# A batched matmul on one core: TensorE's loop takes in the first tile, and a tenth pair of tiles is transposed on VectorE

## The chip, the cores and the metric

One core of one Trainium2 chip runs the whole program. The time is the device time of one execution in microseconds (us), as a median of several runs; the span of a profile is the time from the first to the last instruction of the one execution that was profiled, and is about 1.8 us shorter than that execution's time.

## The reference

```python
batch, m, k, n = 16, 512, 1024, 768
x          # [batch, m, k]  float32, normal
weight     # [k, n]         float32, normal
sub_value  # [batch, m, n]  float32, normal
return (np.matmul(x, weight) - sub_value).astype(np.float32)
```

With batch and m flattened there are 8192 rows, which is 64 **m tiles** of 128 rows. Each tile needs x in 16 bit, transposed (k on the partitions), then 16 weight loads and 16 matmuls of 128x384 (eight slices of k by two halves of n), then the subtraction.

## The kernel before

The kernel is written as one program for each engine, held in step by counting semaphores:

- SyncE (SP) starts all transfers, from one list, in order.
- ScalarE (ACT) casts each x tile to 16 bit, and copies TensorE's transposed tiles out of PSUM, the memory that TensorE writes to ("copy-out").
- For most tiles TensorE (PE) does the transpose: four instructions "T" per tile, two tiles ahead of their matmuls (the prediction writes T for all four). For some **pairs** of tiles VectorE (DVE) does it instead, in 16 instructions that handle 32x32 blocks of both tiles.
- VectorE also does each tile's subtraction, straight from PSUM.

TensorE's program repeats with a period of six tiles, a **lap**: four tiles of its own and one pair of VectorE's.

```python
ON_DVE = frozenset(range(10, 60, 6))     # nine pairs: 10-11, 16-17, ..., 58-59
LEAD_DVE, LEAD_TURN, PER = 7, 5, 6
LOOP = (4, 6, 10)                        # TensorE's loop: from tile 4, 6 tiles, 10 laps

def lead(mi):                            # how many tiles ahead ScalarE casts tile mi
    return LEAD_DVE if mi - mi % 2 in ON_DVE else TA + CA        # 7, else 4
...
for mi in range(HEAD + (EARLY is not None), n_mt):
    ...
    for c in range(n_c):                 # four chunks of k
        matmuls(mi, c)
        if tr:
            tr[c]()                      # one T of tile mi+2 after each chunk; the copy-out follows the fourth
    for t in range(max(mi, ahead), ...):
        if t - lead(t) == mi:
            cast(t)                      # ScalarE, behind the copy-out of this tile
    finish(mi)                           # VectorE's subtraction
    if mi + LEAD_TURN in ON_DVE:
        waiting += transposes_dve(mi + LEAD_TURN)
    for f in waiting[:PER]:              # VectorE: 6, 6 and 4 transposes behind three subtractions
        f()
    del waiting[:PER]
```

The order in which these calls are made is the order of the instructions on each engine. A pair waits for its second cast, TensorE's first weight load of a pair waits for the last of the 16 transposes, and tile t's output slot in PSUM is free when tile t-3 has been subtracted. Ahead of the loop stands a hand-made head that spreads tiles 0 to 2 over the arriving chunks of the weights.

## Time and profile before

| | before |
|---|---|
| time, median of 4 runs | 210.87 us (210.48 to 211.19) |
| span of the profile | 208.9 us |
| TensorE busy / VectorE / ScalarE | 94% / 61% / 52% |
| DMA queue, share of 16 engines | 97.7% |
| bytes moved | 61.87 MB read, 25.17 MB written |
| start of tile 4's matmuls / of tile 10's | 25.61 / 44.00 us |
| one lap in the steady part | 17.34 us |
| end of the matmuls / of the last subtraction / of the span | 201.2 / 202.2 / 208.9 us |

A page gives shares of the whole span, which say who is full but not who waits for whom. So the questions are put to the timeline: what does a lap consist of, and what was each engine released by. The lines are in the prediction below. In them, "[2.08 <-PE po_b L198]" after a row means that the engine had been idle for 2.08 us before it, and that the matmuls of line 198 ended that.

### The profile page before, as it was taken

To read this page: it belongs to the slowest core of one execution; us is meant where nothing else is said; L and a number is where in the kernel's file an instruction comes from. 1 tells how busy PE (TensorE), PEld (TensorE's weight loads), DVE (VectorE), ACT (ScalarE), POOL (GpSimd) and SP (SyncE) were. 2 spreads that over 40 slices of the span, in tenths; PEclk is the share of its full clock that TensorE was granted. 3 is DMA by queue.
4 is the path that set the end of the run, shared out by engine and by line. 5 is a ranking of instruction groups with operands and counts; after the bars stand their busy time and mean duration, and the time that the engine had idled before them with its cause. 6 is when DMAs were issued, how large, how long until landed. Compare 5 with 4: busy or idle time off the path is not lost.

```text
span 208.9 us, 2614 instructions
## 1 busy us (share of the span) xinstructions
PE 196.7 (94%) x1234; PEld 75.4 (36%) x700; DVE 127.8 (61%) x224; ACT 108.8 (52%) x113; POOL 1.0 (0%) x7
## 2 busy tenths in 40 slices
PE   6999799989999999999999999999999999999950
PEld 0234244333434434433443443343344344334310
DVE  2323316955993995596499299369749929943330
ACT  4364768507664671762844767173584655525300
POOL 1000000000000000000000000000000000000000
PEclk9999999999999999999999999999999999999996
DMA  6999999999999999999999999999999999999992
GB/s 238 406 426 433 440 420 436 449 431 430 433 458 414 353 446 445 446 414 411 475 419 422 438 414 438 461 425 422 431 447 397 436 442 438 414 438 442 411 417 119
DMA packets 5620, 87.08 MB, mean 417 GB/s; under 512 B 624, under 2 KB 624, under 8 KB 2032
## 3 DMA queue, kind: packets, MB, share of 16 engines
q1 hardware_dynamic: 5616, 87.03, 97.7%
q8 instruction: 1, 0.02, 0.0%
q14 instruction: 3, 0.02, 0.0%
HBM read 61.87 MB, written 25.17 MB: 417 GB/s over the span
## 4 chain that ended last, share of the span: by engine, by line
PE 72%; DMA 18%; SPq 4%; ACT 1%; issue 1%; DVE 0%
PE po_b L198 65%; DMA x_ring<-in_x_dram 18%; PE pt_b L335 7%; SPq L298 3%; SPq L262 1%; ACT xt_b L348 0%; DVE so_ring L417 0%; ACT x_b L317 0%; SPq L553 0%; ACT x16p_b L317 0%; SPq L138 0%
## 5 line engine op out<-in xcount | busy, mean ns | idle before, releaser
L198 PE MATMUL po_b<-w_sb,xt_b 128*128 128x384 f16 x704 | 126.0, 326 | 0.3 <-ACT xt_b L348 0.2
L417 DVE TENSOR_TENSOR so_ring<-po_b,so_ring 128x768 f32<-128x768 f32 x64 | 60.4, 956 | 58.6 <-PE po_b L198 37.4
L348 ACT COPY xt_b<-pt_b 128x1024 f16<-128x1024 f16 x44 | 44.5, 1012 | 64.2 <-PE pt_b L335 63.2
L368 DVE STREAM_TRANSPOSE xtp_b<-x16p_b 32x256 f32<-32x256 f32 x144 | 62.7, 435 | 3.3 <-ACT x16p_b L317 1.1
L198 PE MATMUL po_b<-w_sb,xtp_b 128*128 128x384 f16 x320 | 61.4, 326 | 1.0 <-DVE xtp_b L368 0.9
L397 PEld LDWEIGHTS <-xt_b 128*128 128x128 f16 x352 | 34.4, 98 | 57.7 <-issue 53.6
L317 ACT CAST x_b<-x_ring 128x1024 f16<-128x1024 f32 x46 | 47.2, 1048 | 4.3 <-DMA x_ring<-in_x_dram 4.3
L335 PE MATMUL pt_b<-ident,x_b 128*128 128x128 f32 x184 | 47.6, 274 | 1.6 <-ACT x_b L317 1.4
L335 PEld LDWEIGHTS pt_b<-ident,x_b 128*128 128x128 f32 x184 | 25.3, 141 | 46.0 <-issue 41.3
L317 ACT CAST x16p_b<-x_ring 128x1024 f16<-128x1024 f32 x18 | 18.8, 1046 | 16.8 <-DMA x_ring<-in_x_dram 16.8
L397 PEld LDWEIGHTS <-xtp_b 128*128 128x128 f16 x160 | 15.7, 98 | 19.9 <-issue 17.8
L265 DVE CAST w_sb<-so_ring 128x768 f16<-128x768 f32 x8 | 4.1, 556 | 11.4 <-DMA so_ring<-in_weight_dram 11.4
L198 PE MATMUL po_b<-idle_x,idle_w 128*128 128x512 f16 x26 | 8.8, 495 | 1.7 <-POOL idle_x L178 1.7
L348 ACT COPY xtp_b<-pt_b 128x1024 f16<-128x1024 f16 x2 | 2.0, 1012 | 2.1 <-PE pt_b L335 2.1
L317 ACT ACT_TABLE_LOAD x1 | 1.3, 1283 | 0.9 <-SPq L138 0.9
L427 PEld LDWEIGHTS <-idle_w 128*128 128x128 f16 x4 | 0.4, 99 | 1.7 <-POOL idle_x L178 1.7
L187 DVE TENSOR_TENSOR ident<-along,across 32x32 f32<-32x32 f32 x4 | 0.7, 183 | 0.1
L179 DVE MEMSET ones<- 128x32 f32 x1 | 0.1, 85 | 1.0 <-SPq L138 1.0
L178 POOL MEMSET idle_x<- 128x512 f16 x1 | 0.5, 528 | 0.0
L499 ACT CAST stub<-ident 128x1 f16<-128x1 f32 x2 | 0.4, 195 | 0.0
L184 DVE STREAM_TRANSPOSE across<-along 128x32 f32<-128x32 f32 x1 | 0.2, 212 | 0.0
L476 POOL MEMSET mark<- 128x1 f32 x1 | 0.1, 99 | 23.6 <-ACT xtp_b L348 23.6
(7 smaller groups left out, 1.0 us busy)
## 6 DMA issues: line engine op xcount, KB each, us to landing
so_ring<-in_sub_value_dram SPq DMA_DIRECT2D x7, 3072.0 KB, 24.2
x_ring<-in_x_dram SPq DMA_DIRECT2D x5, 4096.0 KB, 23.8
out_dram<-so_ring SPq DMA_DIRECT2D x6, 3072.0 KB, 29.2
x_ring<-in_x_dram SPq DMA_DIRECT2D x2, 2048.0 KB, 27.0
so_ring<-in_weight_dram SPq DMA_DIRECT2D x4, 768.0 KB, 8.2
x_ring<-in_x_dram SPq DMA_DIRECT2D x1, 3072.0 KB, 28.6
out_dram<-so_ring SPq DMA_DIRECT2D x1, 2688.0 KB, 26.5
x_ring<-in_x_dram SPq DMA_DIRECT2D x2, 1024.0 KB, 24.8
```

Source lines behind the costliest of these rows:

```text
L178: pool.add(lambda: nc.gpsimd.memset(idle_x, 0.0), then=count("idle"))
L187: dve.add(lambda here=here: nc.vector.tensor_tensor(out=ident[here, here], in0=along[here], in1=across[here], op=mybir.AluOpType.is_equal, ...
L198: return nc.tensor.add_instruction(mybir.InstMatmult(name=nc.get_next_instruction_name(), engine=full.engine, ins=list(full.ins), outs=lis ...
L262: sp.add(lambda st=st, at=at: nc.sync.dma_start(out=st, in_=w_c[at]), then=(sem, 16))
L265: lambda at=at, r=r, st=st: nc.vector.tensor_copy(out=w_sb[:, at, r], in_=st[:, r]),
L298: sp.add(lambda here=here, there=there: nc.sync.dma_start(out=here, in_=there), waits, (sem, 16))
L317: act.add(lambda: nc.scalar.copy(out=to, in_=x_in), waits, count("cast"))
L335: pe.add(lambda: nc.tensor.transpose(words, from_, ident), waits, count("turn") if last else None)
L348: act.add(lambda: nc.scalar.copy(out=to, in_=pt_b[:, b]), waits, count("evac"))
L368: dve.add(lambda: nc.vector.transpose(xt[b * Q : (b + 1) * Q, :, a * Q : (a + 1) * Q], x16[a * Q : (a + 1) * Q, :, b * Q : (b + 1) * Q],), ...
L397: pe.add(lambda weights=weights: nc.tensor.ldweights(weights, tile_position=(0, 0)), [w for w in waits if w[0] in ready])
L417: dve.add(lambda: nc.vector.tensor_tensor(out=o, in0=po[:, :, :NS], in1=o, op=mybir.AluOpType.subtract), [landed["s", mi], (counter["mul"] ...
```

## The change

The intent: a shorter TensorE program (254 instructions, instead of a head, a loop and a tail), in which tile 0 already belongs to the loop. Each turn has a block of four own tiles and a block of the pair; the last turn leaves after the first block. Tiles 4 and 5 become a tenth pair, the hand-made head goes, w2 and w3 are loaded earlier, and the four T of a tile come together, after the third chunk.

A loop in TensorE can wait on a counter only if the counts grow by the same step in every turn. With tile 0 in the loop this means that ScalarE has to cast the tiles in an order which keeps the counter "cast" in step from the first turn on. The change gets that by casting both tiles of a pair at the end of the tile before VectorE begins with them, so that all casts are in the order of the tiles. The diff, shortened and with its lines regrouped:

```diff
-LEAD_DVE = 7
+TURN_AT = 2
 LEAD_TURN = 5
-ON_DVE = frozenset(range(10, 60, 6))
-LOOP = (4, 6, 10)
+PERIOD, ON_PE = 6, 4
+ON_DVE = frozenset(range(4, 60, 6))
 TRANSFERS = [
-    ('x', 0, 1), ('w', 0, 1), ('x', 1, 1), ('w', 1, 1), ('x', 2, 1), ('w', 2, 1),
-    ('x', 3, 2), ('w', 3, 1), ('s', 0, 1), ('x', 5, 3), ('s', 1, 3), ('x', 8, 4), ...
+    ('x', 0, 1), ('w', 0, 1), ('x', 1, 1), ('w', 1, 1), ('w', 2, 1), ('x', 2, 1),
+    ('w', 3, 1), ('x', 3, 1), ('x', 4, 2), ('s', 0, 1), ('x', 6, 2), ('s', 1, 3), ('x', 8, 4), ...
... (emit_loop with one body becomes emit_turns with two blocks and two branches; the head goes) ...
+    casts = {0: [3, 4, 5]}
+    for mi in range(6, n_mt):
+        casts.setdefault(mi - mi % PERIOD + PERIOD - 1 - PERIOD if on_dve(mi) else mi - TA - 2, []).append(mi)
...
         for c in range(n_c):
             matmuls(mi, c)
-            if tr:
-                tr[c]()
+            if c == TURN_AT and mi + TA < n_mt and not on_dve(mi + TA):
+                transpose_tile(mi + TA)
+        for t in sorted(casts.get(mi, [])):
+            cast(t)
         finish(mi)
-        if mi + LEAD_TURN in ON_DVE:
-            waiting += transposes_dve(mi + LEAD_TURN)
-        for f in waiting[:PER]:
+        for t in range(mi + 1, n_mt):
+            if t in ON_DVE and mi == max(t - LEAD_TURN, 0):
+                waiting += transposes_dve(t)
+        for f in waiting[: 16 if mi < PERIOD - 1 else PER]:
             f()
```

## The prediction

> **What bounds the kernel now.** I read the page first, then the chain that ended last in order of time, then the timeline of each engine over the head and over one lap of TensorE's loop (six m tiles). A tile is 128 rows of x; a pair is two tiles whose transpose VectorE does; T is a tile's four TensorE transposes.
>
> ```profile
> PE 196.7 (94%) x1234; PEld 75.4 (36%) x700; DVE 127.8 (61%) x224; ACT 108.8 (52%) x113; POOL 1.0 (0%) x7
> DMA  6999999999999999999999999999999999999992
> ```
>
> Two resources are full at once: TensorE is 94% busy, and the DMA engines are at 90% or more in nearly every slice. VectorE and ScalarE seem to have room, but only on average.
>
> ```profile
> 9.99 38.47 DMA x_ring<-in_x_dram
> ...
> 57.09 5.85 PE po_b L198 x36
> ...
> 74.43 5.85 PE po_b L198 x36
> ...
> 91.78 5.85 PE po_b L198 x36
> ```
>
> The chain hangs on an x transfer until 48.5 us and on TensorE afterwards. The long pieces (tiles that carry no T) return every 17.34 us: that is a lap. It equals the work: 96 matmuls at 0.1625 (4 in 0.65) are 15.6, and 16 transposes at 0.108 (0.758 - 0.65 between their neighbours) are 1.73; sum 17.33. So laps cost nothing but arithmetic. A tile with T takes 3.03 us, one without 2.60. The waits of TensorE's loads between 60 and 201 us are all on "issue", at most 0.3 us each: no data wait is left. A lap moves 6 x (0.524 + 2 x 0.393) = 7.86 MB, at about 433 GB/s 18.15 us, longer than 17.34: the DMA queue carries a backlog, and the matmuls end at 201.2, the last stores at 208.
>
> Now the pair of such a lap, from the timeline of VectorE and TensorE (start, duration, engine):
>
> ```profile
> 68.29 0.96 DVE L417 TENSOR_TENSOR so_ring<-po_b,so_ring 128x768 f32<-128x768 f32 x1 [2.08 <-PE po_b L198]
> 69.16 2.66 DVE L368 STREAM_TRANSPOSE xtp_b<-x16p_b 32x256 f32<-32x256 f32 x6
> 71.84 0.96 DVE L417 TENSOR_TENSOR so_ring<-po_b,so_ring 128x768 f32<-128x768 f32 x1
> 72.83 2.68 DVE L368 STREAM_TRANSPOSE xtp_b<-x16p_b 32x256 f32<-32x256 f32 x6
> 75.53 0.96 DVE L417 TENSOR_TENSOR so_ring<-po_b,so_ring 128x768 f32<-128x768 f32 x1
> 76.52 1.80 DVE L368 STREAM_TRANSPOSE xtp_b<-x16p_b 32x256 f32<-32x256 f32 x4
> ...
> 79.47 0.81 PE L198 MATMUL po_b<-w_sb,xtp_b 128*128 128x384 f16 x4
> ```
>
> VectorE needs 9.16 us for a pair (69.16 to 78.32), with two subtractions in between, and starts right after the subtraction of tile 17. TensorE wants the pair at 79.47. **The slack is only 1.15 us**; the pair's casts were done at 68.32, before they were needed.
>
> **What the Trainium skill says.** (1) "TensorE: Matmul & The Clock Gate", Architectural detail: only TensorE reorders (weight loads), ScalarE and VectorE are strict first in, first out. The trace agrees: ScalarE idled 7.58 us before the cast at 48.49, and a finished TensorE transpose was copied out only afterwards, at 49.44. So program order on those engines counts. (2) The same page, The HAM clock gate: idle for a window of about 3.4 us halves the clock. Here the granted clock fell to 0.50 by 205 us, after the last matmul at 201.2; gaps of 1.4 us around 22 us left it at 1.00. (3) "Runtime: NRT & Kernel Launch", Instruction fetch mechanics: 256 instructions are one fetch block, and a branch out of the resident blocks stalls. The old loop shows no stall (17.34 against 17.33), so a 254-instruction program has nothing to win in the laps. (4) "DMA: Bandwidth & Descriptors", Where 436 GB/s comes from: a ceiling of 435 GB/s. The slices of 420 to 440 agree.
>
> **The change, part by part.**
>
> *Transposes moved.* Tiles 4 and 5 go from TensorE to VectorE: 184 transposes become 176, 8 x 0.108 = 0.9 us less TensorE, 16 x 0.445 = 7.1 us more VectorE.
>
> *T after the third chunk, four in a row.* Same cost (0.43), and the result is ready earlier in the tile.
>
> *The loop* now covers all tiles, with blocks of four and two and two branches a lap. Queued matmuls hide these, as in the old loop: about 0.
>
> *The head.* It no longer spreads tiles 0 to 2 over the arriving weights; w2 and w3 are loaded earlier instead. Transfer times, from the old landings:
>
> ```profile
> 16.94 1.03 DVE L265 CAST w_sb<-so_ring 128x768 f16<-128x768 f32 x2 [3.29 <-DMA so_ring<-in_weight_dram]
> 24.38 2.69 DVE L417 TENSOR_TENSOR so_ring<-po_b,so_ring 128x768 f32<-128x768 f32 x3 [4.55 <-DMA so_ring<-in_sub_value_dram]
> 25.61 0.81 PE L198 MATMUL po_b<-w_sb,xtp_b 128*128 128x384 f16 x4 [0.16 <-issue]
> ```
>
> 5.77 MB had landed at 16.9 and 8.91 at 24.4: 0.425 MB/us. In the new order w3 is in at 4.72 MB = 14.45 us, x4 and x5 at 6.29 MB = 18.15. Tile 0 ends at 16.2 (last w cast 15.5 plus a chunk), tile 1 at 19.2, tile 2 at 21.8, tile 3 at 24.4. But tile 4 needs its pair and, for its output slot, the subtraction of tile 1. ScalarE casts tiles 4 and 5 by 20.2. VectorE then does all 16 transposes in one run, 20.24 + 7.15 = 27.4, and only then subtracts tile 1: 28.4. Tile 4 starts at **28.45 instead of 25.61**: 2.8 us late, after a TensorE gap of 4.0 us.
>
> *The casts of the pairs.* This is the part that I think decides. The old code cast a pair 7 tiles ahead, one cast in each of two tiles. The new code puts both casts at the end of the tile before the one where VectorE begins, behind the copy-out of that tile's T and one other cast. Durations on ScalarE from the old trace:
>
> ```profile
> 17.50 0.60 PE L335 MATMUL pt_b<-ident,x_b 128*128 128x128 f32 x4
> 18.13 1.01 ACT L348 COPY xt_b<-pt_b 128x1024 f16<-128x1024 f16 x1 [1.99 <-PE pt_b L335]
> ...
> 57.18 1.01 ACT L348 COPY xt_b<-pt_b 128x1024 f16<-128x1024 f16 x1 [2.02 <-PE pt_b L335]
> 58.09 1.99 ACT L317 CAST x_b<-x_ring 128x1024 f16<-128x1024 f32 x2
> ...
> 41.96 1.79 DVE L368 STREAM_TRANSPOSE xtp_b<-x16p_b 32x256 f32<-32x256 f32 x4
> ...
> 44.00 0.81 PE L198 MATMUL po_b<-w_sb,xtp_b 128*128 128x384 f16 x4 [0.88 <-DVE xtp_b L368]
> ```
>
> From the start of tile 5 (of tile 11, and so on): 12 matmuls 1.95; T until its copy starts 0.63 (17.50 to 18.13); copy until the first cast 0.91; two casts at a spacing of 0.945, 1.89; the last cast 1.05; hand-over 0.04: VectorE starts at +6.47, where the old order would have let it start at about +4.0 (tile end 3.03 plus a subtraction). Then 9.16 for the pair and 0.25 until a matmul (41.96 + 1.79 to 44.00): +15.88. TensorE would be there at 3 x 3.03 + 2 x 2.60 = +14.3. So it **waits about 1.55 us in each lap**. This does not heal: tile 11 starts 3.03 after tile 10, so the lap is 18.9 us instead of 17.34, a closed ring TensorE, ScalarE, VectorE, TensorE, slower than the DMA's 18.15.
>
> *Sum.* Tile 5 starts at 28.45 + 3.03 = 31.48, tile 10 at 47.35 (old: 44.00), tile 11 at 50.4, tile 59 eight laps later at 201.6. Tiles 59 to 61 (3.03 each) and 62, 63 (2.60) end at 215.9; the old end was 201.2, so 14.7 later. The last subtraction ends at 216.9. In the old run the span ended 6.7 us after it, of which about 3 us were DMA backlog; that backlog is gone, since the DMA has caught up. I take 4.6 us: 3.3 as an empty queue's first load took, 1.4 from landing to the end. Span 221.5, plus 1.8 (210.7 against 208.9): 223.3. I predict **223 us**.
>
> **Rivals.** (a) *DMA stays the bound.* The bytes and their order after x6 are unchanged and DMA is full everywhere; if the new waits hid in its backlog, 208 to 213 us. Against it: 14.7 us is more than the backlog of 3 to 6 us, and the output of the last tile can't go before its matmuls. (b) *Only the head costs*: if the casts came in time, the 2.8 us would partly hide behind x16, which lands at 48.5: 211 to 214. It needs VectorE to start 1.5 us sooner than I compute; the order of the instructions on ScalarE speaks against it. (c) *Better*: 0.9 us of TensorE and fewer instructions to fetch, 208 to 210. TensorE isn't alone on the path, so even without any wait little comes of it. (d) *Worse*: the 4.0 us gap halves the clock for a window (1.7 us), or a branch to the second block misses a fetch; 225 to 228.
>
> **Range and chances.** The per-lap wait is a difference of two sums; an error of 0.4 us in it makes 9 x 0.4 = 3.6 us, and the head is good to 1 us. So 218 to 227.5 us. Slower by over 2% (over 215.1) 0.92; within 2% 0.06; faster 0.02.
>
> **What would show it.** Right: TensorE idles once a lap before the first pair matmul, released by VectorE's transposes; laps of 18.9 us; VectorE's first transposes of a pair released by ScalarE's cast of the pair; a gap of about 4 us before tile 4 with 16 transposes in a row; DMA slices under 90% late in the run; matmuls ending near 216. Wrong: laps of 17.3 or of 18.15 with x loads as releasers, or tile 4 before 27 us.

## The result, and the profile after

| | before | after |
|---|---|---|
| time, median of 4 runs | 210.87 us (210.48 to 211.19) | 223.64 us (222.38 to 223.99) |
| span of the profile | 208.9 us | 220.5 us |
| start of tile 4 / of tile 10 | 25.61 / 44.00 | 28.46 / 47.30 |
| one lap | 17.34 | 18.85 (one of eight: 19.16) |
| end of the matmuls / last subtraction / span | 201.2 / 202.2 / 208.9 | 215.9 / 216.9 / 220.5 |

The changed kernel is slower: ratio 1.06, 95% interval 1.056 to 1.064. (Here and below a ratio is one of mean times, so it is not quite the ratio of the medians.)

The page of the changed kernel, busy times, the DMA engines in 40 slices and the shares of the chain that ended last:

```profile
PE 196.2 (89%) x1217; PEld 71.5 (32%) x691; DVE 135.4 (61%) x240; ACT 105.9 (48%) x109; POOL 0.9 (0%) x6
...
DMA  6999999999999999999999999997999999939085
...
DVE 39%; PE 31%; ACT 16%; DMA 6%; issue 5%; SPq 2%; ACTq 0%
```

TensorE is as long busy as before, in a longer span. The DMA engines, full to the end before, now have slices at 70%, 30% and 0%: they stand still at times, and no longer set the end alone. The chain of before hung on DMA and then on TensorE alone; now VectorE and ScalarE hold more than half of it. VectorE is no busier as a share (61% both times), and still it stands on the path. The waits, in total, times and longest, name the links:

```profile
DVE xtp_b L365 <- ACT x16p_b L320: 21.2, 9, 2.6
...
PE po_b L201 <- DVE xtp_b L365: 12.4, 9, 1.6
```

Nine times VectorE waited for ScalarE's cast of a pair, and nine times TensorE waited for VectorE's transposes of it: once for each of the pairs from 10-11 on. (L345 is the copy-out, L320 the casts, L365 VectorE's transposes, L411 the subtraction, L201 the matmuls.) One lap in the timeline, ScalarE, then VectorE, then TensorE:

```profile
34.13 1.01 ACT L345 COPY xt_b<-pt_b 128x1024 f16<-128x1024 f16 x1 [1.07 <-PE pt_b L338]
35.04 1.05 ACT L320 CAST x_b<-x_ring 128x1024 f16<-128x1024 f32 x1
35.99 1.99 ACT L320 CAST x16p_b<-x_ring 128x1024 f16<-128x1024 f32 x2
...
38.01 2.67 DVE L365 STREAM_TRANSPOSE xtp_b<-x16p_b 32x256 f32<-32x256 f32 x6 [2.33 <-ACT x16p_b L320]
...
45.37 1.80 DVE L365 STREAM_TRANSPOSE xtp_b<-x16p_b 32x256 f32<-32x256 f32 x4
...
47.30 2.11 PE L201 MATMUL po_b<-w_sb,xtp_b 128*128 128x384 f16 x12 [1.34 <-DVE xtp_b L365]
66.15 2.11 PE L201 MATMUL po_b<-w_sb,xtp_b 128*128 128x384 f16 x12 [1.34 <-DVE xtp_b L365]
85.00 2.11 PE L201 MATMUL po_b<-w_sb,xtp_b 128*128 128x384 f16 x12 [1.34 <-DVE xtp_b L365]
104.16 2.11 PE L201 MATMUL po_b<-w_sb,xtp_b 128*128 128x384 f16 x12 [1.65 <-DVE xtp_b L365]
```

The copy-out waits for TensorE's T of this tile; behind it stand one own cast and the two casts of the pair; VectorE, free since 35.7, idles 2.33 us until the second is done at 37.98; it needs 9.16 us (38.01 to 47.17); and TensorE idles 1.34 us before the pair's first matmul. The starts repeat every 18.85 us. In the head, tile 4 starts only when VectorE has done 16 transposes in one run and then the subtraction of tile 1:

```profile
20.24 7.18 DVE L365 STREAM_TRANSPOSE xtp_b<-x16p_b 32x256 f32<-32x256 f32 x16
27.45 2.69 DVE L411 TENSOR_TENSOR so_ring<-po_b,so_ring 128x768 f32<-128x768 f32 x3
...
15.55 5.28 PE L201 MATMUL po_b<-w_sb,xt_b 128*128 128x384 f16 x16 [1.17 <-DVE w_sb L268]
...
28.46 2.11 PE L201 MATMUL po_b<-w_sb,xtp_b 128*128 128x384 f16 x12 [0.99 <-DVE so_ring L411]
```

The row at 15.55 is a surprise: 16 matmuls in 5.28 us are 0.33 us each, half speed. The granted clock was 0.50 from about 14.6 to 21.4 us. It fell after short TensorE gaps of 2.02, 1.04 and 0.42 us, within the one of 1.17. It cost no time here, because tile 4 waits for VectorE anyway; it only turned most of the gap before tile 4 into slower work.

Where the 11.6 us of span come from: tile 10 starts 3.3 us later; the eight laps from there to tile 58 take 151.1 us (7 x 18.85 + 19.16) instead of 139.5 (the first old one was 18.1, tile 16 at 62.1, then 7 x 17.34), 11.6 more; together 14.9, against 14.7 measured at the end of the matmuls. The tail from the last subtraction to the end of the span is 3.6 us instead of 6.7, which gives 3.1 back. (The median time grew by 12.8 us: the profiled run was the fastest of the changed kernel's.)

### The profile page after: what moved, and what is told of

Its sections match the earlier page's. It is cut to its first block, busy times and chain, and to the rows that moved or that the text cites. A ratio compares the mean times of both kernels' runs of the same rounds, so it can differ in the third digit from the quotient of the medians.

```text
span 220.5 us, 2621 instructions
## 1 busy us (share of the span) xinstructions
PE 196.2 (89%) x1217; PEld 71.5 (32%) x691; DVE 135.4 (61%) x240; ACT 105.9 (48%) x109; POOL 0.9 (0%) x6
## 4 chain that ended last, share of the span: by engine, by line
DVE 39%; PE 31%; ACT 16%; DMA 6%; issue 5%; SPq 2%; ACTq 0%
DVE xtp_b L365 31%; PE po_b L201 26%; ACT x16p_b L320 9%; DVE so_ring L411 8%; DMA x_ring<-in_x_dram 6%; PE pt_b L338 4%; ACT x_b L320 4%; ACT xt_b L345 3%; SPq L265 1%; SPq L301 1%; ACTq L55 0%; SPq L506 0%; SPq L143 0%
## 5 line engine op out<-in xcount | busy, mean ns | idle before, releaser
L201 PE MATMUL po_b<-w_sb,xt_b 128*128 128x384 f16 x704 | 122.6, 330 | 2.2 <-DVE w_sb L268 2.2
L345 ACT COPY xt_b<-pt_b 128x1024 f16<-128x1024 f16 x44 | 44.5, 1012 | 97.8 <-PE pt_b L338 97.8
L411 DVE TENSOR_TENSOR so_ring<-po_b,so_ring 128x768 f32<-128x768 f32 x64 | 60.3, 956 | 47.7 <-PE po_b L201 40.7
L365 DVE STREAM_TRANSPOSE xtp_b<-x16p_b 32x256 f32<-32x256 f32 x160 | 69.7, 436 | 23.7 <-ACT x16p_b L320 21.2
L201 PE MATMUL po_b<-w_sb,xtp_b 128*128 128x384 f16 x320 | 56.9, 326 | 13.4 <-DVE xtp_b L365 12.4
L320 ACT CAST x_b<-x_ring 128x1024 f16<-128x1024 f32 x44 | 45.1, 1048 | 5.2 <-DMA x_ring<-in_x_dram 5.2
L338 PE MATMUL pt_b<-ident,x_b 128*128 128x128 f32 x176 | 27.0, 276 | 2.4 <-ACT x_b L320 2.4
L338 PEld LDWEIGHTS pt_b<-ident,x_b 128*128 128x128 f32 x176 | 22.1, 143 | 18.0 <-ACT x_b L320 11.8
L320 ACT CAST x16p_b<-x_ring 128x1024 f16<-128x1024 f32 x20 | 19.9, 1045 | 1.4 <-DMA x_ring<-in_x_dram 1.4
L201 PE MATMUL po_b<-idle_x,idle_w 128*128 128x512 f16 x17 | 5.5, 472 | 1.7 <-POOL idle_x L181 1.7
```

The source lines that it names most:

```text
L201: return nc.tensor.add_instruction(mybir.InstMatmult(name=nc.get_next_instruction_name(), engine=full.engine, ins=list(full.ins), outs=lis ...
L320: act.add(lambda: nc.scalar.copy(out=to, in_=x_in), waits, count("cast"))
L338: pe.add(lambda: nc.tensor.transpose(words, from_, ident), waits, count("turn") if last else None)
L345: act.add(lambda: nc.scalar.copy(out=xt_b[:, d], in_=pt_b[:, b]), waits, count("evac"))
L365: dve.add(lambda: nc.vector.transpose(xt[b * Q : (b + 1) * Q, :, a * Q : (a + 1) * Q], x16[a * Q : (a + 1) * Q, :, b * Q : (b + 1) * Q],), ...
L411: dve.add(lambda: nc.vector.tensor_tensor(out=o, in0=po[:, :, :NS], in1=o, op=mybir.AluOpType.subtract), [landed["s", mi], (counter["mul"] ...
```

## The experiments

The theory: ScalarE's order places the casts of a pair too late, and this closes a ring (TensorE's T, copy-out, three casts, 16 transposes, the pair's matmuls) that is longer than both TensorE's own lap and the DMA's. The rivals: VectorE is overloaded by the tenth pair; the two-block program or its branches cost; the new head costs; ScalarE just has too much to do.

Three of the kernels (e1, e2, e6) need the pairs' casts in another order than that of the tiles. So in these the casts of the pairs count on a semaphore of their own ("castp"), and TensorE waits only on own tiles, whose casts stay in order.

### Control: the semaphore alone (e0_split)

```diff
-        act.add(lambda: nc.scalar.copy(out=to, in_=x_in), waits, count("cast"))
-        cast_at[mi] = so_far["cast"]
+        cast_on[mi] = "castp" if first in ON_DVE else "cast"
+        act.add(lambda: nc.scalar.copy(out=to, in_=x_in), waits, count(cast_on[mi]))
+        cast_at[mi] = so_far[cast_on[mi]]
... (VectorE's pairs wait on "castp"; a reload of x's ring waits on both) ...
```

> Control for the two runs that needed a semaphore of their own for the pairs' casts: the changed kernel with that semaphore and nothing else, ScalarE's order untouched. Theory: the semaphore is neutral, laps of 18.85 us, time 222.5 to 224.5. If the semaphore and not the place of the casts had helped, the time would come down towards 211 to 215.

Measured: 224.39 us (223.78 to 225.11), ratio to before 1.065; laps of 18.85 us, one of 19.16. The semaphore is neutral within 0.4%, where the loss is 6%. In this trace the half clock fell on tile 4 and tile 10 started at 48.62, 1.3 us later than in the profile of the changed kernel. That profile was the fastest of its runs (222.38 us; the others had 223.60 to 223.99), so the same accident may make this difference; it was not traced in those runs.

### The casts seven tiles ahead (e1_casts_seven_ahead)

```diff
 (on top of the control)
-        casts.setdefault(mi - mi % PERIOD + PERIOD - 1 - PERIOD if on_dve(mi) else mi - TA - 2, []).append(mi)
+        casts.setdefault(mi - 7 if on_dve(mi) else mi - TA - 2, []).append(mi)
```

> The changed kernel, but the casts of a VectorE pair come seven tiles ahead, one in each of two tiles, as in the old kernel (they count on a semaphore of their own, so that TensorE's loop can still wait by a fixed step). All else stays: head, ten pairs, two-block loop, four transposes in a row. Theory (casts too late on ScalarE): the wait of 1.3 us before each pair goes, laps of 17.35 us, tile 4 still at 28.5, matmuls end near 202, time 210 to 213, no more than 1% above the old kernel. Rival (VectorE overloaded by the tenth pair, or the two-block program and its branches): laps stay at 18.85 us, time 222 to 224. Rival (the head is what costs): time about 213.7.

Measured: 211.16 us (210.63 to 211.36), ratio 1.0008 (0.999 to 1.0025). The timeline of TensorE:

```profile
28.41 4.00 PE L201 MATMUL po_b<-w_sb,xtp_b 128*128 128x384 f16 x12 [3.85 <-DVE so_ring L415]
...
48.44 2.11 PE L201 MATMUL po_b<-w_sb,xtp_b 128*128 128x384 f16 x12
...
65.79 2.11 PE L201 MATMUL po_b<-w_sb,xtp_b 128*128 128x384 f16 x12
```

No idle time is left before the pairs (no bracket at 48.44 and 65.79), and the lap is 17.35 us. The tenth pair, the head, T in a block, both branches and the 254 instructions are all still there, so none of them is the cause of the longer laps. The gap of 3.85 us before tile 4 is there as well, and tile 4 after it ran at half clock (12 matmuls in 4.00 us instead of 2.11); tile 10 starts 4.4 us later than in the old kernel, the matmuls end at 204.7, 3.5 us later, and the time is the same. So the head's delay is real and costs nothing: it lies inside the DMA's backlog. The matmuls ended later than the expected 202, by this half clock: tiles 4 to 9 took 20.03 us (28.41 to 48.44) instead of 17.35, 2.7 more.

### A smaller dose: the pair ahead of the own cast (e2_pair_before_own)

```diff
 (on top of the control)
-        for t in sorted(casts.get(mi, [])):
+        for t in sorted(casts.get(mi, []), key=lambda t: (mi >= PERIOD - 1 and not on_dve(t), t)):
```

> The changed kernel, the two casts of a pair put ahead of the one own cast of the same tile, still behind that tile's copy-out; own semaphore for the pairs. A smaller dose. Theory: VectorE starts 0.945 us earlier in each lap, the wait of TensorE falls from 1.5 to 0.55 us, laps of 17.9 us; nine laps save 8.5 us of TensorE, matmuls end near 207, time 213 to 215. Rivals (VectorE's load, the program's form): 222 to 224, laps of 18.85.

Measured: 215.56 us (215.35 to 216.77), ratio 1.024, just above the expected 213 to 215. TensorE:

```profile
47.84 2.11 PE L201 MATMUL po_b<-w_sb,xtp_b 128*128 128x384 f16 x12 [0.40 <-DVE xtp_b L369]
65.75 2.11 PE L201 MATMUL po_b<-w_sb,xtp_b 128*128 128x384 f16 x12 [0.40 <-DVE xtp_b L369]
```

The idle time before a pair fell from 1.34 to 0.40 us, and the lap from 18.85 to 17.91: 0.94 us, one cast's spacing, as expected. The half clock met tile 4 here too (12 matmuls in 3.66 us), which is 1.55 us more than the 2.11 of full speed and puts all later tiles back by as much: that is about the miss.

### T after the first chunk (e3_turn_after_first)

```diff
-TURN_AT = 2
+TURN_AT = 0
```

> The changed kernel with one number changed: TensorE's four transposes come after the first of a tile's four chunks, not after the third, so that ScalarE's copy-out, and the casts that stand behind it, come 1.3 us earlier. No cast moves in ScalarE's order. Theory (the ring TensorE transposes, copy, three casts, pair, matmuls): wait per lap 1.5 - 1.3 = 0.2 us, laps of 17.6 us, time 210 to 214. Rival (ScalarE or VectorE simply has too much to do in a lap): no change, 222 to 224.

Measured: 210.84 us (210.69 to 212.45), ratio 1.0022 (0.998 to 1.0064). VectorE's first transposes of a pair in this kernel, and TensorE's first matmuls of tiles 10 and 16:

```profile
54.34 2.68 DVE L365 STREAM_TRANSPOSE xtp_b<-x16p_b 32x256 f32<-32x256 f32 x6 [1.03 <-ACT x16p_b L320]
...
46.09 0.81 PE L201 MATMUL po_b<-w_sb,xtp_b 128*128 128x384 f16 x4
63.64 0.81 PE L201 MATMUL po_b<-w_sb,xtp_b 128*128 128x384 f16 x4
```

Not one instruction of ScalarE moved in its order; only TensorE's T moved to another place in its tile. VectorE's wait for the cast fell from 2.33 to 1.03 us, by 1.30, the two chunks of 0.65 by which T moved. Laps are 17.55 us (46.09 to 63.64), 0.2 above 17.34 as expected, and the time lies in the expected 210 to 214. The load of ScalarE and VectorE is that of the changed kernel, so "too much to do" falls; the ring stands.

### The old kernel with late casts (e4_before_casts_late)

```diff
 (on the kernel before)
     def lead(mi):
-        return LEAD_DVE if mi - mi % 2 in ON_DVE else TA + CA
+        return 5 + mi % 2 if mi >= n_mt or mi - mi % 2 in ON_DVE else TA + CA
...
-            if t - (lead(t) if t < n_mt else LEAD_DVE) == mi:
+            if t - lead(t) == mi:
```

> The old kernel with nothing but the casts of the pairs moved to the tile and place where the changed kernel has them (fifth and sixth tile ahead, behind that tile's copy-out and one own cast). Old head, nine pairs, old loop. Theory: the loss comes by this alone, and a little more than in the changed kernel, since the old copy-out comes 0.65 us later in the tile: laps of 19.6 us, matmuls end near 219.7, time 224 to 228. Rival (new loop, new head or tenth pair cause the loss): the old kernel's time, 210 to 212.

Measured: 233.52 us (232.70 to 234.34), ratio 1.1065. The cause is right, the size was missed by 5.5 us beyond the range. TensorE:

```profile
87.47 0.81 PE L198 MATMUL po_b<-w_sb,xtp_b 128*128 128x384 f16 x4 [2.15 <-DVE xtp_b L368]
...
107.08 1.44 PE L198 MATMUL po_b<-w_sb,xtp_b 128*128 128x384 f16 x4 [2.10 <-DVE xtp_b L368]
...
128.38 0.81 PE L198 MATMUL po_b<-w_sb,xtp_b 128*128 128x384 f16 x4 [2.14 <-DVE xtp_b L368]
```

The lap from 87.47 to 107.08 is 19.61 us, as expected; the next is 21.30. In it four matmuls took 1.44 us instead of 0.81. The stretches of the trace around it (length, busy times of TensorE, its weight loads, VectorE, ScalarE and GpSimd, then the granted clock, DMA share and GB/s):

```profile
105.00:106.00 1.00, 0.00 (x0) 0.00 (x0) 0.94 (x4) 0.00 (x0) 0.00 (x0) 1.00 1.06 459
106.00:107.00 1.00, 0.00 (x0) 0.04 (x1) 0.96 (x3) 0.00 (x0) 0.00 (x0) 1.00 0.69 295
107.00:108.00 1.00, 0.93 (x4) 0.22 (x3) 1.00 (x2) 0.00 (x0) 0.00 (x0) 0.53 0.68 295
...
109.00:110.00 1.00, 1.00 (x5) 0.37 (x2) 0.00 (x0) 0.00 (x0) 0.00 (x0) 0.50 1.21 524
110.00:111.00 1.00, 1.00 (x7) 0.39 (x3) 0.00 (x0) 0.00 (x0) 0.00 (x0) 0.76 1.21 524
```

The clock fell to half at the end of a gap of 2.1 us and stayed there for about 3.4 us (107.06 to 110.5, by the means of these stretches). Of the eight laps three are 19.6 and five 21.3 us: 5 x 1.7 = 8.4 us, which the expectation did not have, and the middle of the expected range, 226, plus 8.4 is 234.4. So this kernel, with the old head, the old loop and nine pairs, loses more than the changed one by nothing but the place of 18 casts (and of two copies of 0.2 us, which only keep a counter in step at the end).

### A longer wait in the changed kernel (e5_extra_cast)

```diff
         for t in sorted(casts.get(mi, [])):
+            if mi >= PERIOD - 1 and on_dve(t) and t % 2 == 0:
+                act.add(lambda: nc.scalar.copy(out=spare, in_=blank), [(counter["idle"], 3)])
             cast(t)
```

The blank tile is one that GpSimd clears at the start: two earlier forms, which copied from x's ring or from an own transposed tile, were found to race.

> The changed kernel with one useless copy on ScalarE (128x1024, about 0.9 us) just ahead of the two casts of each pair: the suspected wait is made longer. Results stay right. Theory: each lap grows by about 0.9 us to 19.8 us, the gap of TensorE before a pair from 1.3 to 2.25 us; by that alone 230 to 231.5 us. In the old kernel with late casts a gap of 2.1 us brought the half clock in five laps of eight, at 1.7 us each; if gaps of that size do this here too, some laps are 21.4 us and the time is 233 to 242. Rival (ScalarE has slack, only its total load matters): 222 to 225.

Measured: 239.70 us (236.80 to 240.13), ratio 1.132.

```profile
72.55 2.11 PE L204 MATMUL po_b<-w_sb,xtp_b 128*128 128x384 f16 x12 [2.29 <-DVE xtp_b L368]
...
92.35 3.78 PE L204 MATMUL po_b<-w_sb,xtp_b 128*128 128x384 f16 x12 [2.29 <-DVE xtp_b L368]
...
113.81 2.11 PE L204 MATMUL po_b<-w_sb,xtp_b 128*128 128x384 f16 x12 [2.29 <-DVE xtp_b L368]
```

The gap grew by 0.95 us to 2.29. Laps are 19.80 us (72.55 to 92.35), or 21.46 where the half clock fell into them (92.35 to 113.81); four of eight were long. One useless copy of some 0.9 us per lap on an engine that is 48% busy costs 16 us.

### Both remedies together (e6_both)

```diff
 (on top of e1_casts_seven_ahead)
-TURN_AT = 2
+TURN_AT = 0
```

> Casts seven tiles ahead and the four transposes after the first chunk, together: is there anything to win over the old kernel once no lap waits? Theory (the DMA engines set the end as soon as the matmuls end before about 205 us): laps of 17.35 us, matmuls end at 202 to 205, time 210 to 211.5, ratio to the old kernel 0.996 to 1.004. Rival (TensorE sets the end in the old kernel, so that eight transposes less, 0.9 us, and the earlier copy-outs show): 208 to 209.9.

Measured: 210.94 us (210.72 to 211.08), ratio 1.0001 (0.9987 to 1.0015), with five rounds. As expected: laps of 17.35 us, matmuls to 203.7. There is nothing to win over the old kernel this way. All runs together show why:

| kernel | last subtraction done | end of the span | tail |
|---|---|---|---|
| before | 202.2 | 208.9 | 6.7 |
| e6_both | 204.7 | 209.2 | 4.5 |
| e3_turn_after_first | 205.3 | 209.0 | 3.7 |
| e1_casts_seven_ahead | 205.7 | 209.3 | 3.6 |
| e2_pair_before_own | 209.9 | 213.5 | 3.6 |
| after | 216.9 | 220.5 | 3.6 |
| e0_split | 218.2 | 221.8 | 3.6 |
| e4_before_casts_late | 228.7 | 232.3 | 3.6 |
| e5_extra_cast | 234.7 | 238.3 | 3.6 |

As long as the last subtraction is done by about 205.5 us the span ends at 209, whatever TensorE does: the DMA engines have 87 MB to move and finish then. Beyond that, every microsecond of TensorE counts, and the tail is the 3.6 us that the last store and the end of the program take by themselves. The old kernel had about 3 us of slack, and the change took 14.7, nearly five times as much.

## Why the prediction was right

It said 223 us, 218 to 227.5; measured were 223.6. Point by point:

- **What bounds.** Right: two full resources and a slack of 1.15 us in the pair. The DMA's bound lies at a span of 209, as e1, e3 and e6 show.
- **The head.** Tile 4 was put at 28.45 us and started at 28.46, by the path named. The gap of 4.0 us before it was not seen in the profile of the changed kernel (0.99), because an earlier half clock, which I had not foreseen, had stretched tile 1 and what follows it; in e1 it was 3.85. That the head alone would cost little (rival b's half of it) is shown by e1: nothing at all.
- **The casts.** VectorE was put at +6.47 us from the start of tile 5 and started at +6.52 (31.49 to 38.01). The wait of about 1.55 us per lap is 1.5 in the lap (18.85 against 17.34), with an idle time of 1.34 in the row (the row before it is drawn 0.16 us past its last matmul's slot, as four matmuls that follow each other at 0.65 are drawn as 0.81). Lap predicted 18.9, measured 18.85. e1 takes the wait away, e3 all but about 0.2 us of it and e2 all but 0.57 (its lap of 17.91), in three ways; e4 brings it and e5 lengthens it.
- **Branches and program size.** Right, by e1: laps of 17.35 with both branches.
- **The sum.** Matmuls to end at 215.9: they ended at 215.9. The tail was mis-sized: 4.6 estimated (its two terms, 3.3 and 1.4, add to 4.7), 3.6 measured, as in five of the experiments. So the span of the profiled run is 220.5 and not 221.5. The median run is 1.3 us longer than that one, perhaps by a half clock at tile 4 as in e0, which rival (d) had named at 1.7 us; it was not traced here. That 223.3 met the median of 223.64 so closely is therefore in part luck: a tail 1.0 us too long stood in for a delay that the sum did not have.
- **Rivals.** (a), DMA stays the bound: fell, slices at 0% and 30%. (b) and (c): fell. (d): its half clock happens (e0, e1, e2, e5 and e6 at tile 4), but it was no 225 to 228.
- **Readings.** The GB/s of the old page do not only lie at 420 to 440: single slices (without the first and the last) show 353 to 475, some above the ceiling of 435 that was cited, so they agree with it as a mean over time (417) and not slice by slice.

Open: in the changed kernel, e0, e2 and e3 one lap of eight, always the one from tile 22 to tile 28, is 0.31 us longer; there the copy-out on ScalarE starts late for no reason that the profile shows.

## What to carry to other kernels

An engine that is half idle can hold the critical path by the place of its instructions alone: before moving a cast or a copy in a strict queue, add up the whole ring, from what releases the instruction ahead of it to the next such release, and compare that sum with the period of the bound. A loop's bookkeeping (here a counter that must grow by a fixed step) may dictate an order that costs more than the shorter program gains; a second counter frees the order. And a small wait before dense matmuls is not just its own length: here a gap of 2.1 us (e4) or 2.29 us (e5) was followed by half of TensorE's clock for about 3.4 us in about half of the laps, and one of 1.34 us never was.

## What the Trainium skill lacked or had wrong

- "TensorE: Matmul & The Clock Gate", Part 1 and the closing table: the page names an idle window of about 3.4 us, and gaps over some 3 us, as what halves the clock. Here shorter gaps were enough: 2.1 us in e4 (five long laps of eight), 2.29 us in e5 (four of eight), and in the head of the changed kernel a run of gaps of which none was longer than 2.02 us. Gaps of 1.34 us, once in each lap of the changed kernel, never were. (Its section on a second failure mode does say that frequent short idles can do this, but gives no lengths.) The half clock lasted about 3.4 us in e4, which agrees with the page's window, and only 1.00 and 0.50 were granted over whole stretches, as it says.
